# Retention core: the fourth block sum goes into the gate tile, and the last head's late chunks keep operands and gates in one place of the transposed rows

## The chip, the cores and the metric

The kernel runs on one core of one Trainium2 chip. The metric is the device time of one execution in microseconds (us). The time of the kernel before is the median of three runs.

## The reference, cut to what matters

The whole program is two layers of a trunk. The first layer mixes with a gated delta network, the second with retention; both end in a convolutional feed-forward net. The change lies in the retention of the second layer:

```
def retention(h, w_in, w_out):
    H, dk, dv, C = 4, 256, 512, 128
    q, k, v, gate = split(h @ w_in)             # SEQ = 1024 rows, D_MODEL = 1024
    q, k = rot(q), rot(k) * dk ** -0.5
    ...
    scores = einsum('bhncd,bhnmd->bhncm', q, k) * dmask
    intra = einsum('bhncm,bhnmv->bhncv', scores, v)
    def step(state, inp):
        q_n, k_n, v_n = inp
        o = einsum('bhck,bhkv->bhcv', q_n, state) * xi
        state = state * gamma_c + einsum('bhck,bhcv->bhkv', k_n * zeta, v_n)
        return state, o
    ...
    o = _standardize(o, 1e-6).reshape(b_, s, H * dv)
    o = o * silu(gate)
    return o @ w_out
```

There are 4 heads of 8 chunks of 128 rows. For each chunk the output `o` (128 rows x 512 values) is standardized by row, multiplied with the gate values, and later multiplied with the output weight `w_out`.

## The kernel before

The engines are TensorE (PE), VectorE (DVE), ScalarE (ACT), GpSimd (POOL) and SyncE (SP); SP issues most of the DMA transfers, ACT some. A scheduler written in the kernel (`run`, called at L2076) interleaves two streams by costs and due times: `ret_fill`, the products that fill TensorE (the values of later heads, then the start of the output projection), and one `core(h)` for each head, which works through the head's chunks. A tile scheduler below it sets semaphores and, when a tile has to take a place that is still in use, puts the instruction behind those that free the place. Each engine then runs its own instructions strictly in the order in which they stand.

In `core(h)` each chunk n makes the state update, the scores and the output `po`, then hands `po` to `ret_back(h, n, po)`. There VectorE takes mean and variance (L1978 `rst`, L1980 `mv`, L1981), GpSimd the power -1/2 of the variance (L1982, `mv`), VectorE normalizes (L1986, `on`), TensorE transposes `on` in four blocks (L719 through `ptr`, `mm`), and VectorE multiplies with the gate values (L2007, `ot` from `mm` and `gt`). The gate values `gt` have been loaded from DRAM (`gd`) by SP at L2002.

The output projection that follows multiplies by blocks in Strassen's way, so it needs sums of blocks. Rows 0 to 511 (chunks n = 0 to 3, called early here) are upper blocks "11" and "12"; rows 512 to 1023 (n = 4 to 7, late) are lower ones. An early chunk stores its two halves as "11" and "12" into DRAM (`od`, L2011, issued by ACT). A late chunk reads the matching early blocks back into the tile `op` (called `pv` as a view, L1998, two loads on SP), stores its own second half as "22" (L2015, on ACT), and then lets GpSimd make four sums, each stored by SP as soon as it is there (L2018 and L2019): "S1" in place in the first half of `ot`, "S2" and "S4" in place in `op`, and "S3" in place in the second half of `ot`, the half that the store "22" reads.

The tiles `op`, `gt` and `ot` of a chunk share the tag `cv`, which has 4 places (`BUFS`, L43). The tag `xT` has 2 places of twice the size. A place is given again once every reader and writer of its tile has ended, transfers included. In head 3, `ret_fill` has reached the output projection: `proj_gen` loads its operands `ar` (L1429, from `od` of earlier heads) and `Bw` and `Br` (L1462, weights) on SP; ACT and VectorE round and split them into `ab` and `bb` (L89, L90), and TensorE multiplies those (`acc` from `bb`, `ab`). Beside it run the steps `xg` of `gain_step` (load L2067, two GpSimd operations, store L2058), one in each early chunk and one in chunk 4 of head 3.

Of the kernel before, what the change touches and what calls it, by code (L numbers as in the profile page):

```python
# [12 lines left out]
ALU = mybir.AluOpType  # L13
AX = mybir.AxisListType

P = 128
# [3 lines left out]
HALF = 512  # L20
NCH = S // P
GH = 8
RH = 4
# [10 lines left out]
def trunk_kernel(ctx: ExitStack, tc, A):  # L34
# [11 lines left out]
    def tl(tag, shape, dt=F32, name=None):  # L46
        return sb.tile(shape, dt, tag=tag, name=name or tag, bufs=BUFS[tag])
# [13 lines left out]
    def mm_tile():  # L61
        return ps.tile([P, HALF], F32, tag="mm", name="mm", bufs=2)
# [13 lines left out]
    def v4(ap):  # L76
        return ap.rearrange("p (c f) -> p c f", f=P)
# [501 lines left out]
    xT = {}  # L579
# [138 lines left out]
    def ptr(out, src):  # L718
        pq(pe.transpose(out, src, ident), 0.109)  # L719
# [4 lines left out]
    def emit(name, lat=0.0):  # L724
        events[name] = clk[0] + lat
# [1205 lines left out]
    def core(h):  # L1931
# [9 lines left out]
        for n in range(NCH):  # L1941
# [25 lines left out]
            if n > 0:  # L1967
                for j in range(2):
                    pm(po, r["q"][j], St[:, j], start=False, stop=(j == 1), cost=0.857)
            give("qkv", 2)  # L1970
            yield [(-0.1, ret_back(h, n, po))]
            yield RL["c"]
            St, r = Sn, rn
        emit(("core", h))

    def ret_back(h, n, po):
        st = tl("st", [P, 2, 6], name="rst")
        dve.bn_stats(st[:, 0], po)  # L1978
        mv = tl("s8", [P, 4], name="mv")
        dve.bn_aggr(mv[:, 0:2], st[:, 0])  # L1980
        dve.tensor_scalar(mv[:, 2:3], mv[:, 1:2], 1e-6, None, ALU.add)  # L1981
        pool.tensor_tensor(mv[:, 3:4], mv[:, 2:3], mhalf[:, 0:1], ALU.pow)  # L1982
        if n < 4 or h == RH - 1 and n == 4:
            gains.pop(0)()
        on = tl("t2", [P, HALF], name="on")
        anchor["on"] = dve.tensor_scalar(on, po, mv[:, 0:1], mv[:, 3:4], ALU.subtract, ALU.mult)  # L1986
        s4 = slice(n % 4 * P, (n % 4 + 1) * P)

        def pair_view(t):
            return t.rearrange("p (j a f) -> p a j f", a=2, f=P)  # L1990

        def blk(nm):
            return od[2 * h:2 * h + 2, ABLK.index(nm), :, s4].rearrange("j p t -> p j t")

        if n > 3:
            pv = pair_view(tl("cv", [P, 516], name="op")[:, 0:HALF])
            for a, nm in enumerate(("11", "12")):
                sp.dma_start(pv[:, a], blk(nm))  # L1998
        yield RL["b"]
        sl = slice(n * P, (n + 1) * P)  # L2000
        g = tl("cv", [P, 516], name="gt")[:, 0:HALF]
        sp.dma_start(v4(g), gd[4 * h:4 * h + 4, :, sl].rearrange("j p t -> p j t"))  # L2002
        pt = mm_tile()
        for j in range(4):
            ptr(pt[:, j * P:(j + 1) * P], on[:, j * P:(j + 1) * P])
        ot = tl("cv", [P, 516], name="ot")[:, 0:HALF]
        dve.tensor_mul(ot, pt, g)  # L2007
        ov = pair_view(ot)
        if n < 4:
            for a, nm in enumerate(("11", "12")):  # L2010
                anchor["x", 1] = act.dma_start(blk(nm), ov[:, a])  # L2011
            if n == 3:
                emit(("ob", h), RL["o"])
            return
        act.dma_start(blk("22"), ov[:, 1])  # L2015
        for d, x, y, op, nm in ((ov[:, 0], ov[:, 0], ov[:, 1], ALU.add, "S1"), (pv[:, 0], ov[:, 0], pv[:, 0], ALU.subtract, "S2"),
                                (pv[:, 1], pv[:, 1], pv[:, 0], ALU.subtract, "S4"), (ov[:, 1], ov[:, 1], pv[:, 0], ALU.subtract, "S3")):
            pool.tensor_tensor(d, x, y, op)  # L2018
            (pool if n == NCH - 1 and h == RH - 1 else sp).dma_start(blk(nm), d)  # L2019

# [159 lines left out]
```

## Time and profile before

| | us |
|---|---|
| median of three runs | 2869.46 (2869.28 to 2872.84) |
| the profiled execution, its own time | 2876.44 |
| its span in the profile | 2874.6 |
| TensorE busy in the span | 2784.8 |
| VectorE busy in the span | 2183.4 |
| ScalarE busy in the span | 1297.3 |
| GpSimd busy in the span | 490.9 |

The mean granted TensorE clock of that execution is 0.994. The retention core lies at 1747 to 2080 us of the span; a head takes about 81 us and a chunk about 9 us. Rows of a timeline give the start in the span, the duration, the engine and line, the tile written and the tiles read, and in brackets how long the engine stood idle before and what ended that. An SP or ACT row with a "q" is the issue of a transfer; when the transfer lands is read from the view of its tile, as the time from issue to landing. Rows of the waits give the engine and line that waited, what it waited for, the total time, the number of times and the longest.

### The profile page before, as it was taken

The page shows a single profiled execution, that of the slowest core. Times are in us where ns is not written, and L with a number is a line of the kernel's source. Part 1 is how long each engine was busy: PE and PEld are TensorE (multiplying, and loading weights), DVE is VectorE, ACT ScalarE, POOL GpSimd, SP SyncE. Part 2 cuts the span into 40 slices and gives each one's busy share as a digit, 9 for nine tenths or more (in the row PEclk, how much of TensorE's full clock was granted, in tenths as well). Part 3 has the DMA queues.
Part 4 walks back from the last instruction along what each step waited for, and adds up shares of the span by engine and source line. Part 5 has one row for each costly group of instructions (what it writes and reads, how often), then busy time and mean ns, then how long its engine had stood idle before and what let it go on. Part 6 is the DMA issues. An engine that isn't in the chain of part 4 may idle for free.

```text
span 2874.6 us, 38923 instructions
## 1 busy us (share of the span) xinstructions
PE 2784.8 (97%) x13594; PEld 2275.9 (79%) x13594; DVE 2183.4 (76%) x3874; ACT 1297.3 (45%) x2387; POOL 490.9 (17%) x517
## 2 busy tenths in 40 slices
PE   8999999999999999999999999999999999999997
PEld 6778878877788778887788887777787788788886
DVE  6787778676788888778687666666789887777869
ACT  4664465343644444546333332222344644445443
POOL 0311321000023233000000002333301033332001
PEclk9999999999999999999999999999999999999999
DMA  7233242174255555945343354665864253444843
GB/s 279 88 96 122 92 133 95 60 246 149 97 189 168 191 184 172 333 128 178 126 147 113 126 198 153 205 188 173 258 210 147 74 194 132 143 137 163 320 149 117
DMA packets 251988, 465.30 MB, mean 162 GB/s; under 512 B 24144, under 2 KB 76752, under 8 KB 251792
## 3 DMA queue, kind: packets, MB, share of 16 engines
q1 hardware_dynamic: 217472, 407.50, 42.8%
q10 hardware_dynamic: 31488, 46.15, 4.4%
q0 software_dynamic: 2832, 9.18, 0.8%
q8 instruction: 107, 1.75, 0.2%
q14 instruction: 89, 0.73, 0.1%
HBM read 346.86 MB, written 115.87 MB: 161 GB/s over the span
## 4 chain that ended last, share of the span: by engine, by line
PE 56%; DVE 21%; DMA 11%; ACT 6%; issue 4%; POOL 1%; SPq 0%; ACTq 0%; DVEq 0%; POOLq 0%
PE acc L716 9%; PE acc L1296 5%; PE acc L110 4%; PE acc L111 4%; PE acc L112 4%; PE sc L716 4%; PE acc L1592 3%; PE sc L1296 3%; DVE o L1743 2%; PE mm L716 2%; DMA mvw<-in_ada_w 2%; DMA wr<-in_ffn_up 2%; DVE wb L90 2%; DVE qkv L490 2%; DVE mm L1350 1%
## 5 line engine op out<-in xcount | busy, mean ns | idle before, releaser
L716 PE MATMUL acc<-hT,wh 128*128 128x512 f32 x960 | 300.1, 394 | 0.0
L1592 PE MATMUL acc<-bb,ab 128*128 128x512 f32 x984 | 231.4, 394 | 7.6 <-DVE ab L90 6.4
L89 ACT ACTIVATE ab<-ar 128x512 fp32r<-128x512 f32 x210 | 131.0, 629 | 216.5 <-PE mm L303 55.1
L1592 PEld LDWEIGHTS acc<-bb,ab 128*128 128x128 f32 x984 | 184.1, 189 | 50.1 <-DVE ab L90 4.8
L716 PEld LDWEIGHTS acc<-hT,wh 128*128 128x128 f32 x960 | 182.9, 190 | 35.7
L1296 PE MATMUL acc<-T,wb 128*128 128x512 f32 x840 | 202.0, 389 | 0.4 <-DVE wb L90 0.4
L90 DVE TENSOR_TENSOR ab<-ar,ab 128x512 fp32r<-128x512 f32 x210 | 149.1, 718 | 68.9 <-ACT ab L89 68.7
L716 PE MATMUL acc<-hT,wl 128*128 128x512 f32 x480 | 197.2, 411 | 2.4 <-ACT sq L509 2.4
L89 ACT ACTIVATE wb<-mm 128x512 fp32r<-128x512 f32 x216 | 124.3, 597 | 166.3 <-DVE mm L1350 154.7
L1296 PEld LDWEIGHTS acc<-T,wb 128*128 128x128 f32 x840 | 157.5, 188 | 33.8 <-ACT o L1744 1.2
L90 DVE TENSOR_TENSOR wl<-wr,wh 128x1024 fp32r<-128x1024 f32 x98 | 124.3, 1268 | 76.6 <-ACT wh L89 71.9
L89 ACT ACTIVATE wh<-wr 128x1024 fp32r<-128x1024 f32 x98 | 103.8, 1060 | 137.0 <-PE acc L716 49.6
L90 DVE TENSOR_TENSOR wb<-wr,wb 128x512 fp32r<-128x512 f32 x162 | 115.4, 714 | 64.7 <-ACT wb L89 64.7
L1774 POOL TENSOR_TENSOR o<-o 128x512 f32<-128x512 f32 x80 | 114.5, 1439 | 266.8 <-ACT pc L1366 173.9
L1743 DVE SCALAR_TENSOR_TENSOR o<-g,vc,o 128x512 f32<-128x512 f32 (+2 forms) x176 | 151.5, 871 | 8.4 <-ACT o L1738 7.2
L90 DVE TENSOR_TENSOR wb<-mm,wb 128x512 fp32r<-128x512 f32 x216 | 144.4, 681 | 7.4 <-ACT wb L89 7.4
L89 ACT ACTIVATE wb<-wr 128x512 fp32r<-128x512 f32 x162 | 101.2, 626 | 92.8 <-PE acc L1296 28.0
L1350 DVE TENSOR_TENSOR mm<-wr 128x512 f32<-128x512 f32 x108 | 83.8, 776 | 73.3 <-DMA wr<-in_ffn_up 59.3
L716 PE MATMUL acc<-wh,hT 128*128 128x512 f32 x384 | 134.4, 412 | 1.7 <-DVE vv L90 1.7
L1366 ACT ACTIVATE pc<-acc 128x512 f32<-128x512 f32 x143 | 84.3, 590 | 110.7 <-PE acc L1296 63.5
L239 DVE SCALAR_TENSOR_TENSOR ada<-mvw,e,ada 128x512 f32<-128x512 f32 x140 | 105.3, 752 | 26.0 <-DMA mvw<-in_ada_w 25.7
L110 PE MATMUL acc<-T,wb 128*128 128x512 f32 x292 | 114.4, 392 | 4.8 <-DVE wb L90 4.8
(677 smaller groups left out, 7340.2 us busy)
## 6 DMA issues: line engine op xcount, KB each, us to landing
wr<-in_ffn_up SPq DMA_DIRECT2D x92, 512.0 KB, 4.0
mvw<-in_ada_w SPq DMA_DIRECT2D x80, 512.0 KB, 4.5
ad<-o SPq DMA_DIRECT2D x154, 256.0 KB, 2.3
ar<-ad SPq DMA_DIRECT2D x154, 256.0 KB, 4.3
Br<-in_ffn_down SPq DMA_DIRECT2D x88, 256.0 KB, 5.2
wr<-in_ret_wv SPq DMA_DIRECT2D x32, 512.0 KB, 3.7
ar<-od SPq DMA_DIRECT2D x56, 256.0 KB, 4.9
wr<-in_gdn_wqkv SPq DMA_DIRECT2D x24, 512.0 KB, 3.6
```

The source lines that it names most:

```text
L89: anchor["sp"] = act.activation(dst_h, src, AF.Copy)
L90: eng.tensor_tensor(dst_l, src, dst_h, ALU.subtract)
L110: mm(acc, wl[:, k], hl[0], start=first, stop=False)
L111: mm(acc, wh[:, k], hl[1], start=False, stop=False)
L112: mm(acc, wh[:, k], hl[0], start=False, stop=last)
L239: dve.scalar_tensor_tensor(a, wr[:, kk], e[:, k:k + 1], a, ALU.mult, ALU.add)
L716: pq(pe.matmul(out, lhsT, rhs, start=start, stop=stop), cost or COST[out.shape[-1]])
L1296: return pe.matmul(*a, skip_group_check=True, **kw)
L1350: dve.tensor_tensor(t, x, y, op)
L1592: return pe.matmul(*args, skip_group_check=True, **kw)
L1743: dve.scalar_tensor_tensor(tv, gv[:, c0 - j:c1 - j], w[:, 2 - j:3 - j], tv, ALU.mult, ALU.add)
L1774: (dve if fp == 0 else pool).tensor_tensor(o[d], o[x], o[y], op)
```

## The change

Two edits in `ret_back`. In every late chunk the fourth sum "S3" is written into the first block pair of the gate tile `gt`, whose values the product has used up by then, and is stored from there; the second half of `ot` is no longer overwritten. And in the late chunks of head 3 alone, `op` and `gt` are the two halves of one tile `home` of the tag `xT`, so that there only `ot` takes a place of `cv`.

```
+        late = h == RH - 1 and n > 3
+        home = tl("xT", [P, 2, HALF], name="op") if late else None
         if n > 3:
-            pv = pair_view(tl("cv", [P, 516], name="op")[:, 0:HALF])
+            pv = pair_view(home[:, 0] if late else tl("cv", [P, 516], name="op")[:, 0:HALF])
             for a, nm in enumerate(("11", "12")):
                 sp.dma_start(pv[:, a], blk(nm))
         yield RL["b"]
         sl = slice(n * P, (n + 1) * P)
-        g = tl("cv", [P, 516], name="gt")[:, 0:HALF]
+        g = home[:, 1] if late else tl("cv", [P, 516], name="gt")[:, 0:HALF]
...
-                                (pv[:, 1], pv[:, 1], pv[:, 0], ALU.subtract, "S4"), (ov[:, 1], ov[:, 1], pv[:, 0], ALU.subtract, "S3")):
+                                (pv[:, 1], pv[:, 1], pv[:, 0], ALU.subtract, "S4"), (pair_view(g)[:, 0], ov[:, 1], pv[:, 0], ALU.subtract, "S3")):
```

Two lines are added above, so L2002, L2018 and L2019 of before are L2004, L2020 and L2021 of the changed kernel, and L1998 is L2000. The order on TensorE is the same in both. Since places become free at other points, SP's order moves. The first place is heads 0 to 2; here is SP in head 0, from chunk 4's stores to chunk 6's gate load. Before (`gt<-gd` is a gate load, `od<-ot` and `od<-op` are stores of sums, `op<-od` is the re-read of early blocks, `qk` a load for the next head):

```order
L2002 DMA gt<-gd 128x4x128
L2019 DMA od<-ot 128x2x128
L2019 DMA od<-op 128x2x128 x2
L2019 DMA od<-ot 128x2x128
L2026 DMA qk<-qd 128x512 x2
L1998 DMA op<-od 128x2x128 x2
L2019 DMA od<-ot 128x2x128
L2002 DMA gt<-gd 128x4x128
L2019 DMA od<-op 128x2x128 x2
L2019 DMA od<-ot 128x2x128
```

and in the changed kernel:

```order
L2021 DMA od<-ot 128x2x128
L2021 DMA od<-op 128x2x128 x2
L2021 DMA od<-gt 128x2x128
L2004 DMA gt<-gd 128x4x128
L2028 DMA qk<-qd 128x512 x2
L2000 DMA op<-od 128x2x128 x2
L2021 DMA od<-ot 128x2x128
L2021 DMA od<-op 128x2x128 x2
L2021 DMA od<-gt 128x2x128
L2004 DMA gt<-gd 128x4x128
```

The gate loads of chunks 5 and 6 (and 7) stood ahead of the stores of the sums of the chunk before, or between them; now each stands behind the last of them, and its place is that of the product tile `ot` of the chunk before. The same holds in heads 1 and 2. The second place is SP in head 3's early chunks, where the output projection's loads begin. Before (`xg` are the gain steps' loads and stores, `ar` and `Bw` the projection's operands):

```order
L2067 DMA xg<-xs_67 128x512
L2002 DMA gt<-gd 128x4x128
L2058 DMA xg_160<-xg 128x512
L2067 DMA xg<-xs_67 128x512
L2002 DMA gt<-gd 128x4x128
L2058 DMA xg_160<-xg 128x512
L1429 DMA ar<-od 128x512
L1462 DMA Bw<-in_ret_wout 128x512
```

and in the changed kernel (`op<-gd` is the gate load into the tile `home`):

```order
L2069 DMA xg<-xs_67 128x512
L2004 DMA gt<-gd 128x4x128
L2000 DMA op<-od 128x2x128
L2060 DMA xg_160<-xg 128x512
L2000 DMA op<-od 128x2x128
L2004 DMA op<-gd 128x4x128
L2069 DMA xg<-xs_67 128x512
L2004 DMA gt<-gd 128x4x128
L2000 DMA op<-od 128x2x128
L2060 DMA xg_160<-xg 128x512
L2000 DMA op<-od 128x2x128
L1429 DMA ar<-od 128x512
```

The loads of chunk 4's and chunk 5's early blocks, and one gate load, now stand ahead of the projection's first operands; each of these blocks is one that chunk 0 or chunk 1 of the same head stores. The third place is GpSimd in head 3's late chunks 4 and 5. Before:

```order
L2018 TENSOR_TENSOR op<-op 128x2x128
L1982 TENSOR_TENSOR mv<-mv,mhalf 128x1
L2018 TENSOR_TENSOR ot<-ot,op 128x2x128
L2018 TENSOR_TENSOR ot<-ot 128x2x128
L2018 TENSOR_TENSOR op<-ot,op 128x2x128
L2018 TENSOR_TENSOR op<-op 128x2x128
L2018 TENSOR_TENSOR ot<-ot,op 128x2x128
L1982 TENSOR_TENSOR mv<-mv,mhalf 128x1
```

and in the changed kernel (`op<-ot,op` directly behind `op<-op` is the fourth sum, in the gate's half of `home`):

```order
L2020 TENSOR_TENSOR op<-op 128x2x128
L2020 TENSOR_TENSOR op<-ot,op 128x2x128
L1982 TENSOR_TENSOR mv<-mv,mhalf 128x1
L2020 TENSOR_TENSOR ot<-ot 128x2x128
L2020 TENSOR_TENSOR op<-ot,op 128x2x128
L2020 TENSOR_TENSOR op<-op 128x2x128
L2020 TENSOR_TENSOR op<-ot,op 128x2x128
L1982 TENSOR_TENSOR mv<-mv,mhalf 128x1
```

The fourth sum of chunk 4 has come ahead of the power `mv` of the next chunk; elsewhere GpSimd's order stays, with another tile written.

## The prediction

> **What bounds the kernel now.** The page comes first: one engine fills the span.
>
> ```profile
> span 2874.6 us, 38923 instructions
> PE 2784.8 (97%) x13594; PEld 2275.9 (79%) x13594; DVE 2183.4 (76%) x3874; ACT 1297.3 (45%) x2387; POOL 490.9 (17%) x517
> ```
>
> TensorE (PE) is busy for 97% of 2874.6 us, so a change pays only where PE stands idle, or costs only where it makes PE idle. The edited lines run in the retention core alone. The table of windows over that core (five stretches from 1747 to 2080 us; the last stretch and the sum) says how much there is to win.
>
> ```profile
> 2030.00:2080.00 50.00, 46.83 (x206) 35.28 (x205) 34.84 (x60) 16.50 (x32) 19.31 (x24) 1.00 0.82 251
> sum 333.00, PE 326.12 PEld 249.81 DVE 223.47 ACT 84.22 POOL 117.66; mean PE 65.22 PEld 49.96 DVE 44.69 ACT 16.84 POOL 23.53
> ```
>
> PE is busy 326.12 of 333.00 us; 6.88 us is all that any edit here can win, and 3.17 of it lies in the last 50 us, where head 3 ends. Which waits make it up, the waits of 1747 to 2080 us say (engine and line, what ended the wait, total, times, longest):
>
> ```profile
> POOL ot L2018 <- DMA od<-ot: 25.4, 16, 2.7
> DVE on L1986 <- POOL mv L1982: 24.8, 23, 4.0
> PE mm L719 <- DVE on L1986: 2.7, 4, 1.2
> PE sc L716 <- DVE on L1986: 2.5, 4, 1.5
> PE acc L716 <- DVE vv L90: 0.8, 3, 0.3
> PE acc L716 <- DVE ab L90: 0.8, 1, 0.8
> ```
>
> The first row is the target: 16 times, once in each late chunk, GpSimd (POOL) waits for a store of the product tile `ot` before the fourth sum, 25.4 us in all. GpSimd is in order, and the small power `mv` (L1982) of the next chunk stands behind that sum, `on` (L1986) behind `mv`, PE behind `on`. But PE lost only 2.7 + 2.5 us to `on`, and the longest wait of the `sc` row stands elsewhere in head 2:
>
> ```profile
> 1946.09 0.96 PE L716 MATMUL sc<-vv,kz 128*128 128x512 f32 x3 [1.54 <-DVE on L1986]
> ```
>
> That is an early chunk, which has no fourth sum. So 25.4 us of waiting are worth 2.7 + 2.5 − 1.5 = 3.7 us to PE.
>
> **The change, part 1: the fourth sum writes into the gate tile (16 late chunks).** The sum's wait goes, its 0.74 us stays. In heads 0 to 2 the gain is what PE loses once a head after chunk 4: the `sc` row less its longest, (2.5 − 1.5) / 3 = 0.3 us a head. The price: the gate tile is now held until the fourth store lands, so the next gate load takes the place of the last product tile and must wait until that tile's two stores ("22" and "S1") have landed. A loop arises that was not there: product, S1 store, its landing, gate load, its landing, next product. Its terms are in head 0's timeline (start, duration; SP rows are issues), the products of the same chunks 4 and 6 in heads 1 and 2, and the landing times of the two tiles in the window (min/median/max; first `ot` stores, then `gt` loads).
>
> ```profile
> 1793.10 0.68 DVE L2007 TENSOR_TENSOR ot<-mm,gt 128x512 f32<-128x512 f32 x1
> 1797.60 0.74 POOL L2018 TENSOR_TENSOR ot<-ot,op 128x256 f32<-128x256 f32 x1 [1.33 <-DMA od<-ot]
> 1801.64 0.69 DVE L2007 TENSOR_TENSOR ot<-mm,gt 128x512 f32<-128x512 f32 x1
> 1803.22 0.36 SPq L2019 DMA_DIRECT2D od<-ot  x1
> 1804.76 0.70 DVE L1978 BATCH_NORM_STATS2 rst<-sc 128x6 f32<-128x512 f32 x1 [2.23 <-PE sc L716]
> 1811.23 0.67 DVE L2007 TENSOR_TENSOR ot<-mm,gt 128x512 f32<-128x512 f32 x1
> 1812.37 1.37 DVE L90 TENSOR_TENSOR vv<-acc,vv 128x512 fp32r<-128x512 f32 x2 [0.19 <-ACT vv L89]
> 1816.11 0.68 DVE L90 TENSOR_TENSOR vv<-acc,vv 128x512 fp32r<-128x512 f32 x1
> 1873.98 0.68 DVE L2007 TENSOR_TENSOR ot<-mm,gt 128x512 f32<-128x512 f32 x1
> 1892.32 0.67 DVE L2007 TENSOR_TENSOR ot<-mm,gt 128x512 f32<-128x512 f32 x1
> 1957.75 0.69 DVE L2007 TENSOR_TENSOR ot<-mm,gt 128x512 f32<-128x512 f32 x1
> 1976.15 0.67 DVE L2007 TENSOR_TENSOR ot<-mm,gt 128x512 f32<-128x512 f32 x1
> DMA to landing us min/median/max: 1.8/3.6/6.5
> DMA to landing us min/median/max: 2.8/4.2/6.3
> ```
>
> One turn of the loop, with medians: 1803.22 − 1801.64 = 1.58 from product to S1's issue, 3.6 to its landing, 4.2 for the gate load, and about 0.1 for the two releases: 9.5 us. Chunk 4's product is as early as before (its gate load waits for nothing new), so chunk 6's comes two turns later, 19.0 us. Before, the same two steps took 1811.23 − 1793.10 = 18.13, 1892.32 − 1873.98 = 18.34 and 1976.15 − 1957.75 = 18.40 us. Chunk 5's own lateness goes into the 2.23 us that VectorE (DVE) idles before `rst` at 1804.76. Chunk 6's has no such cushion: from 1811.23 DVE runs without a pause but for 0.19 us up to the `vv` at 1816.11, for which PE already waits (the `vv` row of the waits: 3 times, one a head). So PE is later by 19.0 − 18.13 − 0.19 = 0.68, 0.47 and 0.41 us: **+1.5 us** over the three heads. These differences are against the old times, so the 0.3 us a head won earlier is in them already: a loop that hides gives 3 × (−0.3) = −1.0. Upwards, with both landings at 4.9 (between the medians and the maxima) a turn is 1.58 + 4.9 + 4.9 + 0.1 = 11.5 and a head loses 23.0 − 18.3 − 0.2 = 4.5. I take the medians, since they are of these transfers in these windows; ends −1.0 and +13.5. Chunk 7's product is later still, but stands before nothing PE waits for soon: I cost it at 0, up to +1 for the three heads if the weight loads behind it in SP's order run late.
>
> [...]
>
> **Part 2: head 3's front.** There `op` and `gt` of the late chunks sit in a place of the tag `xT`, free early, and SP's order now has the loads of chunk 4 and 5's `op` among the early chunks, ahead of the `ar` and `Bw` loads of the output projection. They read blocks that chunk 0's and 1's stores have just written, so SP blocks until these land, with everything behind it. Before, in head 3 (ACTq is the Scalar queue's store issue, SPq the loads' issue):
>
> ```profile
> 2003.07 0.32 SPq L2058 DMA_DIRECT2D xg<-xg  x1
> 2011.53 0.42 SPq L1429 DMA_DIRECT2D ar<-od  x1
> 2012.91 0.90 ACTq L2011 DMA_DIRECT2D od<-ot  x2
> 2016.74 0.62 ACT L89 ACTIVATE ab<-ar 128x512 fp32r<-128x512 f32 x1
> 2017.78 0.62 ACT L89 ACTIVATE ab<-ar 128x512 fp32r<-128x512 f32 x1
> 2021.84 0.68 DVE L90 TENSOR_TENSOR ab<-ar,ab 128x512 fp32r<-128x512 f32 x1
> 2020.93 0.93 PE L716 MATMUL acc<-bb,ab 128*128 128x512 f32 x3
> ```
>
> Chunk 1's stores go out at 2012.91; with the least landing of the window, 1.8, plus the second store's issue and two loads' issues (about 1 us), `ar` goes out near 2016 rather than 2011.53: 4.5 us later. The `ab` on ScalarE at 2016.74 can move to about 2019 and still serve PE's `acc` at 2020.93; the second, at 2017.78, can be 4.06 − 0.62 = 3.4 us later before DVE's `ab` at 2021.84 moves. 4.5 − 3.4 = 1.1 at most, and some of the loads waited in their queue before as well: I take **+0.8 us**, ends 0 (all of it in the slack) and +3 (chunk 1's stores land after the median 3.6 instead of 1.8, +1.8 on top of 1.1).
>
> **Part 3: head 3's late chunks.** Here the wait does reach PE.
>
> ```profile
> 2056.84 0.72 POOL L2018 TENSOR_TENSOR ot<-ot,op 128x256 f32<-128x256 f32 x1 [2.17 <-DMA od<-ot]
> 2058.05 0.42 SPq L2002 DMA_DIRECT2D gt<-gd  x1
> 2058.11 0.81 DVE L1986 TENSOR_SCALAR on<-sc,mv 128x512 f32<-128x512 f32 x1 [4.03 <-POOL mv L1982]
> 2058.98 0.66 PE L719 MATMUL mm<-cst,on 128*128 128x128 f32 x4 [1.24 <-DVE on L1986]
> 2061.06 0.69 DVE L2007 TENSOR_TENSOR ot<-mm,gt 128x512 f32<-128x512 f32 x1 [0.94 <-PE acc L716]
> 2063.16 0.81 DVE L1986 TENSOR_SCALAR on<-sc,mv 128x512 f32<-128x512 f32 x1 [1.13 <-POOL mv L1982]
> 2064.12 0.63 PE L719 MATMUL mm<-cst,on 128*128 128x128 f32 x4 [1.07 <-DVE on L1986]
> 2067.58 2.71 PE L716 MATMUL acc<-bb,ab 128*128 128x512 f32 x9 [0.76 <-DVE ab L90]
> ```
>
> The sum at 2056.84 loses its 2.17 us wait, so `on` at 2058.11 comes over 2 us sooner, and PE's 1.24 us go. The gate load of 2058.05, behind the fourth store on SP, goes ahead as well, so the product of 2061.06 and the `on` of 2063.16 move up and the 1.07 us go. The 0.76 us at 2067.58 come from DVE being late by the same pair of steps; part may stay. All three are 3.07; late next is the load of operands for chunk 6, now behind the fourth store of chunk 4. I take **−2.3 us**, ends −3.1 and −0.5 (the loads land just late).
>
> Nothing else changes in count or size: same matrix products in the same order, same four sums, same transfers. Sum: +1.5 + 0.8 − 2.3 = 0.0 us on the profiled execution's 2876.44 us (span 2874.6). The median of the runs is 2869.46, 7 us below that execution; I carry the difference of 0 over to it and say **2869.5 us**.
>
> **The rivals.**
> (a) *The reload loop sets the pace: slower.* The mechanism of part 1 with slower landings. It decides from the point at which store and load of a turn take together more than 7.8 us (3.6 + 4.2): every 0.1 more costs 2 turns × 3 heads × 0.1 = 0.6 us. To be slower by over 5.7 us, they must take about 8.8. For it: the maxima of 6.5 and 6.3 us. Against: the loads now come at a quieter moment, not beside four stores. With both at 4.9 us: 13.5 − 1.5 = 12.0, so 2881.5 us; around the edge, 2875.
> (b) *SP blocks in head 3's front and PE starves for `ab`.* +3 in place of +0.8: 2871.7 us; with head 3's gain also only −0.5: 2873.5.
> (c) *The loop hides and head 3's stalls all go: a little faster.* −1.0 + 0 − 3.1 = −4.1: 2865.4 us. For it: the same-sized stores landed in 1.8 at best. It is the most that the waits above leave.
> (d) *The wait removed was hidden, and the new ones are too.* The 25.4 us of GpSimd's waits gave PE a few us only; the time would be 2869.5 as in my forecast, but with PE's waits in head 3 unchanged.
>
> **How the numbers follow.** A measurement of this kernel tells about 0.2%, 5.7 us, from no change: 2863.7 to 2875.2. Forecast (terms near the sum's): 0.50; (d) 0.08; (c) 0.17; (b) 0.13; (a) 0.12. No case reaches 2863.7 by its own terms; 0.03 for faster by a cause not seen here. Slower: most of (a), 0.09, and a little of (b), 0.01. The range goes from (c)'s 2865.4 to (a)'s edge at 2875.0; it leaves out most of (a) and the tails.
>
> **What would show it.** In the changed kernel's waits the row of the fourth sum on `od<-ot` is gone, near 0 of 25.4 us. In heads 0 to 2, DVE's product in chunks 5 and 6 waits for the DMA `gt<-gd`, 0.3 to 1 us each; if that row is not there, (c) holds, and if it is 2 us or more a head, (a). In head 3, SP's first `ar` goes out near 2016, and PE's 1.24 and 1.07 us are gone. I am wrong if PE's idle time over the core moves from 6.88 us by more than 4, or if the time moves with PE's idle there unmoved.

## The result

| | before | changed |
|---|---|---|
| first comparison: median of 20 runs each | 2871.69 (2865.1 to 2878.36) | 2876.43 (2870.7 to 2880.9) |
| ratio, first comparison | | 1.0015 (1.0008 to 1.0022) |
| ratio, second (11 runs, 33 of before) | | 0.9998 (0.9989 to 1.0007) |
| ratio, third (11 runs, 35 of before) | | 1.0007 (0.9997 to 1.0017) |
| profiled execution, its own time | 2876.44 | 2875.87 |
| its span | 2874.6 | 2874.1 |

The first comparison makes the kernel slower by 0.15%, about 4 us. Its median lies 6.9 us above the forecast of 2869.5 and 1.4 us above the end of the range (2875.0). Of the 6.9 us, 2.2 are the kernel before, whose median was that much higher there than in the three runs the prediction started from; 2.15 are found below in the retention core of the profiled execution; for the other 2.6 no run here shows a cause. Repeated twice, the comparison gave less. Weighted by runs, the three make (20 x 1.0015 + 11 x 0.9998 + 11 x 1.0007) / 42 = 1.0008, about 2.4 us, still inside the 0.2% that the prediction called no change. So what has to be explained is a small loss where a sum of zero was forecast.

The two spans hardly differ, because the two executions also differ where nothing was edited: the changed one reaches the core 1.63 us sooner and takes 1.02 us less behind it. So the core is measured by itself, by the start times of TensorE's instructions. The page's first lines and the two windows shown of before are, for the changed kernel:

```profile
span 2874.1 us, 38907 instructions
PE 2786.2 (97%) x13594; PEld 2277.2 (79%) x13594; DVE 2182.6 (76%) x3874; ACT 1297.1 (45%) x2387; POOL 483.6 (17%) x517
...
2030.00:2080.00 50.00, 47.14 (x194) 35.69 (x193) 32.24 (x57) 15.62 (x30) 18.01 (x24) 0.93 0.83 266
sum 333.00, PE 325.23 PEld 250.43 DVE 221.01 ACT 83.76 POOL 112.49; mean PE 65.05 PEld 50.09 DVE 44.20 ACT 16.75 POOL 22.50
```

TensorE idles 7.77 us in place of 6.88. But the granted clock of the last stretch (the third figure from the right) is 0.93, where it was 1.00 before. Busy time is then no measure of work done: in rows further below, 3.41 us of it hold 10 products at a clock of 0.50 and 19 at 1.00. The waits of 1747 to 2085 us answer to those of before:

```profile
DVE on L1986 <- POOL mv L1982: 14.7, 20, 1.4
DVE ot L2009 <- DMA gt<-gd: 5.2, 2, 2.7
PE acc L716 <- DVE vv L90: 1.6, 3, 0.6
PE acc L716 <- DVE ab L90: 4.0, 2, 2.9
PE mm L719 <- DVE on L1986: 0.4, 2, 0.2
```

The edit did what it says: the 25.4 us of GpSimd's waits for the store of `ot` have no row any more, `on` waits 14.7 us for GpSimd in place of 24.8, and TensorE's 2.7 us before the transposes have become 0.4. One row is new, the product's waits for gate loads, 5.2 us. Two have grown: TensorE waits 4.0 us for `ab`, in two waits, where it was 0.8 in one, and 1.6 us for `vv` where it was 0.8.

Where the core gains and loses is read from the start times of the same TensorE instructions in both traces:

| landmark on TensorE | before | changed | changed less before |
|---|---|---|---|
| first transposes of `on`, head 0 | 1755.91 | 1754.28 | -1.63 |
| first transposes, head 3 | 2002.52 | 1999.72 | -2.80 |
| chunk 3's transposes, head 3 | 2030.32 | 2028.99 | -1.33 |
| chunk 6's transposes, head 3 | 2058.98 | 2056.19 | -2.79 |
| chunk 7's transposes, head 3 | 2064.12 | 2060.04 | -4.08 |
| next `acc` that had to wait | 2067.58 | 2065.57 | -2.01 |
| first product of L301 | 2087.12 | 2087.64 | +0.52 |

The steps of the last column tell the story: heads 0 to 2 gain 1.17 us (0.22 of it at an early chunk that the edits do not touch, whose 1.54 us wait was 1.32 here), head 3's front loses 1.47, its late chunks gain 1.46 + 1.29 and then lose 2.07 at one wait, and 2.53 more go between the last two landmarks, where TensorE waits for nothing. The core, from the first landmark to the last, went from 331.21 to 333.36 us: +2.15.

**The wait at the end.** TensorE in head 3 of the changed kernel, at the front and at the end:

```profile
2019.54 0.96 PE L716 MATMUL acc<-bb,ab 128*128 128x512 f32 x3 [1.16 <-DVE ab L90]
...
2056.19 0.60 PE L719 MATMUL mm<-cst,on 128*128 128x128 f32 x4
...
2060.04 0.60 PE L719 MATMUL mm<-cst,on 128*128 128x128 f32 x4
...
2065.57 6.79 PE L716 MATMUL acc<-bb,ab 128*128 128x512 f32 x16 [2.86 <-DVE ab L90]
```

The waits of 1.24 and 1.07 us before the transposes are gone. In their place one wait of 2.86 us stands. VectorE says why: four steps on the weights `Br`, the fourth late.

```profile
2059.77 2.99 DVE L1471 TENSOR_TENSOR Bw<-Br,Bw 128x512 f32<-128x512 f32 x3
2064.22 0.69 DVE L1471 TENSOR_TENSOR Bw<-Br,Bw 128x512 f32<-128x512 f32 x1 [1.47 <-DMA Br<-in_ret_wout]
2064.83 0.68 DVE L90 TENSOR_TENSOR ab<-ar,ab 128x512 fp32r<-128x512 f32 x1
```

That load is SP's at 2059.39. SP had stood before it, from 2054.83 to 2057.23 (SP's timeline, then the row of SP's waits from 2050 to 2062):

```profile
2052.98 1.34 SPq L2021 DMA_DIRECT2D od<-op  x1
2054.41 0.42 SPq L1462 DMA_DIRECT2D Br<-in_ret_wout  x1
2057.23 1.02 SPq L2000 DMA_DIRECT2D op<-od  x2
2058.29 0.47 SPq L2004 DMA_DIRECT2D op<-gd  x1
2058.80 0.54 SPq L1429 DMA_DIRECT2D ar<-od  x1
2059.39 0.43 SPq L1462 DMA_DIRECT2D Br<-in_ret_wout  x1
```

```profile
SPq L2000 <- DMA od<-op: 2.3, 1, 2.3
```

`xT` has two places. Chunk 7's tile takes that of chunk 5, which is free when the fourth sum's store, issued at 2052.98, has landed 4.2 us later. Until then SP stands at chunk 7's re-read of L2000, and the `ar` and `Br` loads behind it, which have nothing to do with it, stand too. Before the change both stood ahead of chunk 7's re-read. They were hardly earlier for that: counted from chunk 3's transposes, this `Br` load went out after 29.78 us before and after 30.40 in the changed kernel. What has come forward, by 2.75 us up to chunk 7's transposes, is the work ahead of the product, and the load could not follow.

**The clock behind it.** In the records of this trace the 15 changes of the granted clock lie whole multiples of 3.413 us apart, within 0.002 us. Here are the five stretches of that length around the wait (behind the comma TensorE's busy time and the number of its products, third from the right the granted clock):

```profile
2057.91:2061.32 3.41, 3.41 (x19) 2.79 (x18) 2.33 (x4) 2.98 (x6) 3.33 (x5) 1.00 0.80 223
2061.32:2064.74 3.42, 1.39 (x7) 0.79 (x5) 1.95 (x3) 1.44 (x3) 0.89 (x1) 1.00 0.89 271
2064.74:2068.15 3.41, 2.58 (x6) 1.88 (x7) 3.41 (x6) 0.00 (x0) 1.11 (x1) 0.50 0.61 168
2068.15:2071.56 3.41, 3.41 (x10) 2.63 (x9) 2.15 (x3) 0.24 (x1) 3.02 (x5) 0.50 0.91 278
2071.56:2074.98 3.42, 3.42 (x17) 2.80 (x16) 1.48 (x3) 1.65 (x4) 2.05 (x3) 1.00 0.92 288
```

TensorE is busy for all of 2068.15 to 2071.56 and gets through 10 products, where the full stretches before and behind have 19 and 17. The half clock lasts 6.8 us. TensorE works in 6.0 of them, which at half clock is an estimated loss of 3.0 us; the landmarks show 2.53. Before, the three shorter waits at this place had the clock at 1.00 throughout.

### The profile page after: what moved, and what is told of

The parts are those of the page before. It is cut to its first block, busy times and chain, and to the rows that moved or that the text cites. A ratio compares the mean times of both kernels' runs of the same rounds, so it can differ in the third digit from the quotient of the medians.

```text
span 2874.1 us, 38907 instructions
## 1 busy us (share of the span) xinstructions
PE 2786.2 (97%) x13594; PEld 2277.2 (79%) x13594; DVE 2182.6 (76%) x3874; ACT 1297.1 (45%) x2387; POOL 483.6 (17%) x517
```

## The experiments

The theory, A: SP stands at chunk 7's re-read, `Br` comes late, one long wait of TensorE results, and half clock follows a wait of this length. The rivals: B, the reload loop in heads 0 to 2 makes the loss; C, the half clock is chance. Later D and E came, on whether the loss is real.

**Chunk 7 back in cv.** One step of SP's order differs from the changed kernel.

```
-        late = h == RH - 1 and n > 3
+        late = h == RH - 1 and 3 < n < 7
```

> Both edits, but chunk 7 of head 3 keeps its operand and gate tiles in the tag cv; only chunks 4, 5 and 6 use the place of xT. SP's order differs from the changed kernel's at one point: chunk 7's re-read and gate load stand behind the next pair of ar and Br loads instead of ahead of it. Theory A (SP stands at chunk 7's re-read until chunk 5's place is free, the Br load behind it comes late, TensorE stands 2.86 us at 2062.7 and then runs at half clock for 6.8 us): the stall at the end of head 3 falls to under 1.2 us, the granted clock stays 1.00 from 2040 to 2080, and the time falls by about 4 us against the changed kernel, to a ratio to before of 0.9990 to 1.0005. Theory B (the reload loop in heads 0 to 2 makes the loss): ratio as for the changed kernel, about 1.0015, since the loop is untouched. Theory C (the half clock there is chance and not tied to the stall): the stall goes, but the ratio falls by 0.0005 to 0.001 at most, or the half clock comes without a stall over 1.5 us.

Measured: 0.9993 (0.9983 to 1.0003). SP, VectorE and TensorE there:

```profile
2051.45 0.38 SPq L1462 DMA_DIRECT2D Br<-in_ret_wout  x1
2051.89 0.94 SPq L2000 DMA_DIRECT2D op<-od  x2
...
2056.11 3.59 DVE L1471 TENSOR_TENSOR Bw<-Br,Bw 128x512 f32<-128x512 f32 x4
...
2060.35 2.01 PE L716 MATMUL acc<-bb,ab 128*128 128x512 f32 x6 [1.28 <-DVE ab L90]
...
2040.00:2080.00 40.00, 38.62 (x170) 30.16 (x169) 30.08 (x46) 14.81 (x28) 15.91 (x19) 1.00 0.89 291
```

`Br` goes out ahead of chunk 7's re-read, 26.13 us after chunk 3's transposes in place of 30.40, the four steps run without a break, the wait is 1.28 us (slightly over the 1.2 expected), and the clock from 2040 to 2080 is 1.00. A holds; B does not, since the loop is the same.

**The same on a chip beside the changed kernel**, whose third comparison this was:

> Both edits, with chunk 7 of head 3 in cv, a second time, beside the changed kernel on the same chip. Theory A: the stall before the product of bb and ab at the end of head 3 is 1.0 to 1.5 us, with no half clock there; the ratio lies 0.0007 to 0.0017 under that of the changed kernel in this comparison. Theory E: within 0.0005 of it.

Measured: 0.9990 (0.9981 to 0.9998), 0.0017 under the changed kernel's 1.0007 there, the end of what A expected. The wait is 1.30 us, and the core 328.68 us against 334.11 for the changed kernel. Not all of these 5.43 us are the edit's: 2.36 lie ahead of head 3, nearly all at the untouched early chunk of head 2, which in the changed kernel's trace had a wait of 1.93 us with half clock behind it (1.18 without, here). Head 3 alone, from its first transposes to the first product of L301, took 83.34 us against 86.41.

**Only chunks 6 and 7 in the place of xT** (`n > 5` in the same line).

> Both edits, but only chunks 6 and 7 of head 3 use the place of xT. The re-reads of chunks 4 and 5 then do not stand ahead of the first ar loads, and chunk 7's place is not one that chunk 5 holds. Theory A: neither the 1.16 us stall at 2019.5 nor the 2.86 us stall, clock 1.00 from 2040 to 2080, TensorE idle from 1747 to 2080 about 4 us; ratio to before 0.9985 to 1.0000. Theory B: 1.0010 to 1.0015, as the loop is untouched. Theory C: like A in stalls, with a ratio of 1.0005 or more.

Measured: 0.9994 (0.9985 to 1.0002), in A's range. The front wait is gone and the last one is 1.10 us. A new one came: chunk 5's product waits 3.63 us up to 2051.79, and TensorE behind it 1.94 us for chunk 6's `on`; with these, and 2.08 us at head 2's early chunk, TensorE's idle time is about 7 us and not the 4 expected. The row puts the product's wait down to an `ar` load, but that one, issued at 2046.51, landed after 4.3 us, at 2050.8. The gate load that the product reads, issued at 2046.94, landed after 4.7, at 2051.7, so the wait is for the gate load, which in this kernel is part of the reload loop. No half clock follows there.

**The first edit alone** (the fourth sum into the gate tile in all heads, all tiles in `cv`).

> The first edit alone: the fourth sum goes into the gate tile in all heads, and head 3's tiles stay in cv, so that the reload loop runs in all four heads and nothing of head 3 goes to xT. Theory A: heads 0 to 2 as in the changed kernel (TensorE idle up to 1985 within 0.5 us of it), no front stall at 2019; in head 3 the loop makes the gate loads later and stalls of 1 to 2 us come at its end; no stall over 2 us, clock 1.00; ratio 0.9995 to 1.0010. Theory B: 1.0015 or more, with the loss in heads 0 to 2 and again in head 3. Theory C: no statement beyond the stalls.

Measured: 1.0005 (0.9997 to 1.0014), in A's range, but the stalls were misjudged: none over 2 us was expected, and in head 3, where the projection's loads share SP, the loop makes the product wait, and TensorE behind it for longer than in any other run but one.

```profile
2059.45 0.69 DVE L2007 TENSOR_TENSOR ot<-mm,gt 128x512 f32<-128x512 f32 x1 [4.29 <-DMA gt<-gd]
```

```profile
2062.45 0.87 PE L719 MATMUL mm<-cst,on 128*128 128x128 f32 x3 [4.18 <-DVE on L1986]
```

So the reload loop of the prediction's rival (a) does set the pace in head 3, where the second edit keeps it out. Half clock follows from 2062, 3.4 us of it.

**The second edit alone** (the fourth sum stays in `ot`).

> The second edit alone: head 3's late chunks have operands and gates in the place of xT, and the fourth sum stays in the product tile. SP's front order is that of the changed kernel, and chunk 7's re-read stands ahead of the same ar and Br loads, but chunk 5's place is free once the gate is used and the second and third sums have landed, without the fourth. Theory A: a front stall of 0.5 to 1.2 us before a product of bb and ab near 2019; GpSimd's waits for the product's store stay (1 to 1.3 us at TensorE in chunk 6); chunk 7's re-read on SP waits less, and the last stall is under 2 us, with the clock at 1.00; ratio 0.9998 to 1.0010. Theory B: 0.9995 to 1.0003, since the gate loads of heads 0 to 2 are as before.

Measured: 1.0016 (1.0007 to 1.0025), the highest ratio of the kernels tried. B's 0.9995 to 1.0003 is out: without the loop in heads 0 to 2 there is still a loss. A's numbers missed too, the ratio, the last stall and the clock as well as two more: the front wait was 0.44 us, and TensorE's wait for chunk 6's `on` is gone although the fourth sum still goes to `ot`, since GpSimd waited there only 0.33 us for the store. The expectation that SP waits less was wrong. SP stands at chunk 7's re-read for 4.3 us in place of 2.3 (SP, VectorE, TensorE):

```profile
2054.67 0.47 SPq L1462 DMA_DIRECT2D Br<-in_ret_wout  x1
2059.42 0.87 SPq L2000 DMA_DIRECT2D op<-od  x2
...
2061.51 0.49 SPq L1462 DMA_DIRECT2D Br<-in_ret_wout  x1
...
2066.32 0.69 DVE L1471 TENSOR_TENSOR Bw<-Br,Bw 128x512 f32<-128x512 f32 x1 [2.27 <-DMA Br<-in_ret_wout]
...
2067.67 1.82 PE L716 MATMUL acc<-bb,ab 128*128 128x512 f32 x3 [3.65 <-DVE ab L90]
```

Here chunk 5's third sum holds the place: its store is issued at 2053.56 and lands 5.8 us later. A longer stand of SP, a longer wait (3.65 us), 6.8 us of half clock, a higher time: the mechanism of A, in a larger dose (beside 1.97 us with half clock at head 2's early chunk in this trace).

**The first edit in heads 0 to 2 alone** (head 3 as before).

> The first edit in heads 0 to 2 alone; head 3 as before the change. Theory A (the reload loop is hidden in heads 0 to 2, as the trace of the changed kernel shows): from the first transposes of head 0 to those of head 3 the core is about 1 us shorter than before, ratio 0.9990 to 1.0003. Theory B (the reload loop makes the loss): 1.0010 or more, with the transposes of head 3 later than before by 3 us or more against those of head 0.

Measured: 1.0003 (0.9994 to 1.0012), the upper end of A's range. The time alone does not exclude a small loss. By the transposes, the core up to head 3 is 248.50 us against 246.61 before, longer and not shorter; but that holds a wait of 2.70 us, with half clock, at the untouched early chunk of head 2 (1.54 before, without). Around it, head 0 took +0.06, head 1 −0.13 and head 2's late half −0.85 us, which are the changed kernel's +0.04, −0.13 and −0.86 once more. TensorE's wait for `vv` behind chunk 6's product is 0.62, 0.62 and 0.33 us in the three heads (0.23, 0.22 and 0.33 before), and the waits saved in chunk 5 outweigh that. In head 3, which is as before the change, TensorE's wait of 1.24 us for chunk 6's `on` did not come: GpSimd waited 0.34 us for the store of `ot` there, not 2.17. So that wait hangs on how late one store lands, and not all of its disappearing in the changed kernel need be the edit's.

**Both edits in head 3 alone, chunk 7 in cv.**

> Both edits in head 3 alone, with chunk 7 in cv; heads 0 to 2 as before the change. Theory A: end of head 3 as in the run with chunk 7 in cv (stall 1.0 to 1.5 us, clock 1.00 there). From the first transposes of head 0 to those of chunk 0 of head 3 the core is about 1 us longer than with the first edit in all heads, since the waits of chunk 5 for the product's store come back. Ratio 0.9993 to 1.0002. Theory B (the reload loop costs time in heads 0 to 2): the ratio falls under that of the run with chunk 7 in cv by 0.0003 or more.

Measured: 0.9995 (0.9987 to 1.0004); last wait 1.27 us. From the first transposes of head 0 to those of head 3 it took 2000.30 − 1753.78 = 246.52 us, with the first edit in all heads 1997.64 − 1752.30 = 245.34. Of these 1.18 us 0.49 are the untouched early chunk's (1.67 against 1.18), so 0.7 us of A's 1 are there, and B's sign is wrong.

**A wait made on purpose.** The kernel before, with chunk 6's normalization in head 3 repeated on VectorE.

```
+        if h == RH - 1 and n == 6:
+            for _ in range(2):
+                dve.tensor_scalar(on, po, mv[:, 0:1], mv[:, 3:4], ALU.subtract, ALU.mult)
```

> The kernel before, with the normalization of chunk 6 of head 3 done three times in place of once (two more instructions of 0.81 us on VectorE behind the same power, the result unchanged). TensorE's wait of 1.24 us at 2058 becomes about 1.24 + 1.62 = 2.9 us, the length of the long stall of the changed kernel; the two waits behind it may shrink. Theory A: half clock in the records within 3 us of the stall, and a time of before plus 1.6 plus 2 to 3 us, ratio 1.0010 to 1.0016. Theory C: the clock stays at 1.00 there, and the ratio is 1.0000 to 1.0006.

Measured: 1.0006 (0.9997 to 1.0016). The wait came out at 1.65 us, not 2.9 (GpSimd's wait ahead of it was 1.09 us and not 2.17), so this run did not test the clock at 2.9 us; it shows that 1.65 us left it at 1.00. With four repeats:

> The kernel before, with four more normalizations of chunk 6 of head 3 on VectorE (the result unchanged), two more than in the run with two, where TensorE's wait there was 1.65 us with no half clock near it. Now it is 1.65 + 2 x 0.81 = 3.3 us. Theory A with the clock: half clock for 3 to 7 us within 3 us of that stall; the time 1.6 us above the run with two by the work, and 2 to 3 us more by the clock, so a ratio to before of 1.0015 to 1.0025. Theory C: clock 1.00 from 2040 to 2080, ratio 1.0008 to 1.0013.

Measured: 1.0008 (0.9999 to 1.0017), under the range of A and at its rival's lower end. TensorE and the clock:

```profile
2060.10 1.11 PE L719 MATMUL mm<-cst,on 128*128 128x128 f32 x4 [4.21 <-DVE on L1989]
...
2055.88:2059.29 3.41, 0.01 (x1) 0.00 (x0) 3.34 (x6) 0.00 (x0) 0.00 (x0) 1.00 0.93 287
2059.29:2062.71 3.42, 2.61 (x8) 2.24 (x9) 2.46 (x7) 0.00 (x0) 1.19 (x2) 0.50 0.55 179
2062.71:2066.12 3.41, 3.41 (x9) 2.64 (x8) 3.41 (x4) 1.58 (x3) 3.06 (x4) 0.50 0.70 201
```

The half clock came with the wait, made by nothing but VectorE's extra work, so the trace speaks against C. The time does not settle its price: the ratios of the two runs differ by 0.0002, less than their intervals. The traces give one: from chunk 6's transposes to the first product of L301 it took 28.28 us with four repeats and no wait, and 27.30 us with two, 1.17 of them a wait, so an estimated 2.1 us go to the half clock.

**The changed kernel again, twice, and the kernel before as a new one.**

> The changed kernel once more, unaltered, beside the others on one chip. Theory A (a stall of 2.9 us at the end of head 3, made by SP standing at chunk 7's re-read, and the half clock behind it): the stall comes again at 2.5 us or more before the same product of bb and ab, and the granted clock is 0.50 for 3 to 7 us right behind it; ratio to before 1.0008 to 1.0020. Theory C (the half clock there is chance): stall again, but the clock between 2040 and 2080 at 1.00, or the ratio near 1.0005.

> The changed kernel a third time, since its first two comparisons (1.0015 and 0.9998) lie further apart than their intervals allow for one effect. The core's length in the two traces, from the first transpose of head 0 to the first product of L301, was 2.15 and 1.45 us over that of before. Theory A (stall and half clock at the end of head 3, worth 1.5 to 2.5 us net): the stall again at 2.8 us or more with half clock behind it, the core 1 to 3 us longer than before, ratio 1.0003 to 1.0012. Theory D (the loss of 4 us is real, and more of it lies outside the core): ratio 1.0012 or more. Theory E (no change in time): 0.9996 to 1.0003.

> The kernel before, as if it were a new one: what two sets of runs of one program differ by. If runs scatter independently, the ratio is 1.0000 within 0.0009. If sets of runs differ by something of their own, it lies off by as much as the two comparisons of the changed kernel do, 0.0008 or more.

Measured: 0.9998 (0.9989 to 1.0007), 1.0007 (0.9997 to 1.0017) and 1.0001 (0.9991 to 1.0011). The waits were 2.81 and 2.85 us, at the same product, each with 3.4 us of half clock behind it (6.8 in the first trace). So the stall is there every time; the length of the half clock varies. In time, the second comparison fell in E's range, under A's, and the third in A's. The kernel before against itself is off by 0.0001, though its interval does not exclude 0.0008. The cores were 333.36, 332.66 and 334.11 us for the changed kernel, 331.21 and 332.77 for before: means 333.4 and 332.0. D is not borne out. These lengths hold the waits at head 2's early chunk, which come and go (1.18 to 2.70 us, with half clock or without). Head 3 alone is clearer: 87.92, 86.50 and 86.41 us in the changed kernel, 84.60 and 85.69 before, 83.29 and 83.34 with chunk 7 in `cv`. Whether the loss of the whole kernel is 1 or 3 us these runs do not settle.

## Why the prediction was wrong

**The range and the sum.** The step that failed is part 3, the end of head 3: it counted the waits that go and put at nothing the one that comes, TensorE's 2.86 us for a `Br` load behind chunk 7's re-read, with half clock behind it. The sum of 0.0 was 2.15 us on the profiled core. 2.53 us of it, the half clock, had no term at all. The three parts make −0.95 + 1.47 − 0.68 = −0.16 (−0.22 more is the untouched early chunk), close to their forecast of 0.0 by luck, since they err in both directions.

- *Part 1, +1.5 us for the reload loop in heads 0 to 2*: wrong in sign; 0.95 us were won. The term that was mis-sized is the 4.2 us for a gate load. The six gate loads of chunks 5 and 6 in heads 0 to 2, now issued behind the stores and not beside them, landed in 2.7 to 3.0 us, as the prediction had argued against its rival (a). Head 0's products, its gate loads for chunks 5 and 6, and the landing times of the four gate loads in this stretch (min/median/max; the last is for head 1) show the loop closing in time:

```profile
1791.48 0.68 DVE L2009 TENSOR_TENSOR ot<-mm,gt 128x512 f32<-128x512 f32 x1
1796.14 0.36 SPq L2004 DMA_DIRECT2D gt<-gd  x1
1799.70 0.69 DVE L2009 TENSOR_TENSOR ot<-mm,gt 128x512 f32<-128x512 f32 x1
1804.82 0.36 SPq L2004 DMA_DIRECT2D gt<-gd  x1
1809.29 0.67 DVE L2009 TENSOR_TENSOR ot<-mm,gt 128x512 f32<-128x512 f32 x1
1817.91 0.69 DVE L2009 TENSOR_TENSOR ot<-mm,gt 128x512 f32<-128x512 f32 x1 [2.66 <-DMA gt<-gd]
...
DMA to landing us min/median/max: 2.7/2.9/4.0
```

  The load of 1796.14 landed after 2.9 us and that of 1804.82 after 2.7, so a turn from product to landed gate took 7.5 and 7.8 us, not 9.5, and chunks 5 and 6 did not wait; their products are 17.81 us apart over two chunks, not 19.0. Chunk 7's product does wait, 2.66 us in head 0 and 2.55 in head 1. TensorE's `vv`, for which it waits in heads 0 and 1 some 0.4 us longer than before (0.62 against 0.23 and 0.22), comes ahead of that product. What is longer there is a split of weights on VectorE (head 0, before and changed):

```profile
1814.97 1.21 DVE L90 TENSOR_TENSOR wl<-wr,wh 128x1024 fp32r<-128x1024 f32 x1
1813.04 1.61 DVE L90 TENSOR_TENSOR wl<-wr,wh 128x1024 fp32r<-128x1024 f32 x1
```

  Head 1 has the same 1.21 and 1.61, head 2 has 1.21 both times and no longer wait; why it is longer stays open. That the 0.95 lies at the −1.0 of rival (c) is in part luck: (c) has 0.3 us in each head, and the heads gave +0.04, −0.13 and −0.86 (from chunk 4's to chunk 5's transposes alone −0.31, −0.53 and −0.58).
- *Part 2, +0.8 us at head 3's front*: right in mechanism; in the first trace too small in size. SP waited 10.3 us at the two re-reads, the first `ar` went out at 2013.76 (this trace runs 2.8 us ahead there, so 2016.6 by the times of before, against the 2016 predicted), and TensorE waited 1.16 us; the landmarks give +1.47, inside the ends 0 and +3. In the two later traces of the changed kernel it was +0.75 and +0.91, so the size was about right.

```profile
SPq L2000 <- DMA od<-ot: 10.3, 2, 5.2
...
2013.76 0.49 SPq L1429 DMA_DIRECT2D ar<-od  x1
...
2018.79 0.69 DVE L90 TENSOR_TENSOR ab<-ar,ab 128x512 fp32r<-128x512 f32 x1 [1.47 <-ACT ab L89]
```

- *Part 3, −2.3 us at head 3's end*: the waits named did go (−1.46 and −1.29). But 2.07 came back, so −0.68, near the end of −0.5: inside the range, with a mechanism that was not the forecast's. The prediction asked what is late next and named the operands of chunk 6. It did not ask who stands behind SP when a re-read has to wait for its place. That is the question it had put for the front, in part 2, and not again for the end.
- *The clock*: no term, no rival. Busy and idle time were added up as if a microsecond of waiting cost the same whether it comes in three pieces or one. Here the one piece cost 2.5 us more than its length (in the two later traces 1.6 each, by the same two landmarks). What lacked is the granted clock, which the profile gave for every stretch and which stood at 1.00 there before. The trace of before had a warning outside the core: at 1361.53 TensorE had waited 2.09 us, and from 1362.79 to 1366.21 its clock is 0.50.

The signs that the prediction named held in the main: the row of the fourth sum is gone, TensorE's 1.24 and 1.07 us are gone, the first `ar` went out where it said, and TensorE's idle time moved by less than 4 us, 0.89. One did not: products that wait 0.3 to 1 us for the gate load in chunks 5 and 6. There are none; the row is there for chunk 7 only. "If the time moves with PE's idle there unmoved" is what happened, and the cause was the granted clock.

## What to carry to other kernels

When a tile moves into a tag with few places, look up the instruction that now waits for the place, and then everything that stands behind it on its queue: it is the unrelated load behind it that is late. Here one more place for the last tile (chunk 7 back in `cv`) turned a loss of about 0.08% into a gain of about 0.08%, near the limit of what these runs can tell. When waits are taken away, ask what the work that moves forward will then wait for. Add up waits by length as well as by sum, and read the granted clock beside busy time, since a gathered wait can be dearer than the scattered ones that it replaces: here one of 2.86 us cost 2.5 us beyond its length, where those of 1.24, 1.07 and 0.76 us before had the clock at 1.00.

## What the runs showed of the hardware

In the retention core of these traces the granted clock fell to 0.50 for 3.4 us or twice that at a time, each time with one of the longer waits of TensorE. At the end of head 3 waits of 2.81, 2.85, 2.86, 3.65, 4.18 and 4.21 us each came with it, at the latest 3 us after their end; waits of 1.65, 1.94 and shorter never. At an early chunk of head 2, waits of 2.46, 2.62 and 2.70 us were followed by it, 1.70 and shorter not, and between 1.9 and 2.3 us it went either way (1.93, 1.97 and 2.08 with, 2.02 and 2.29 without).

What set the two kinds apart near 2 us can be read from the traces. In all 14 of them the changes of the clock lie whole numbers of 3.413 us apart, within 0.01 us, so each trace can be divided into stretches of 3.41 us with every change at an end of one. In the core the two kinds differ in how much of a wait fell into one stretch. Here a wait of 1.93 us lies in one (the changed kernel's third trace), and a longer one of 2.29 us is parted between two (the first edit alone, where the clock stays at 1.00 behind it too):

```profile
1938.54:1941.95 3.41, 1.48 (x7) 0.91 (x6) 2.75 (x6) 0.00 (x0) 0.55 (x1) 1.00 0.74 252
1941.95:1945.37 3.42, 3.42 (x15) 3.13 (x14) 3.42 (x7) 0.47 (x1) 0.00 (x0) 0.50 0.64 185
...
1939.23:1942.64 3.41, 2.21 (x10) 1.50 (x8) 1.60 (x4) 1.06 (x1) 0.98 (x2) 1.00 0.95 341
1942.64:1946.05 3.41, 2.32 (x15) 2.14 (x16) 3.18 (x5) 0.47 (x1) 0.19 (x1) 1.00 0.12 28
```

In the cores of the 14 traces (1747 to 2090 us) TensorE stood idle for 1.93 us or more in 12 such stretches, and each is followed by one at 0.50; of the 1366 others at full clock, with 1.65 us at most, none is. A second stretch at 0.50 followed where TensorE was idle for 0.80, 0.83 and 1.06 us of the first, into which the wait reached; with 0.34 us or less it did not. So the wait of 2.86 us in the changed kernel, which left 0.83 us of idle time in the first stretch at 0.50, had 6.8 us of half clock, and those of 2.81 and 2.85 us had 3.4. The 1.93 us do not carry over to the rest of the program: before the change, a stretch at 509.46 us with 0.81 us idle is followed by 0.50. What lies behind the lengths these runs do not show.
